# A recurrence's opening: where a background inverse is issued, and when one load is

## The chip, the cores and the metric

The kernel runs on one core of a Trainium2 chip. The metric is the device time of one execution in microseconds (us); lower is better. The engines of the core are TensorE (PE), VectorE (DVE), ScalarE (ACT), GpSimd (POOL) and SyncE (SP, which issues most DMAs). Each works through its own queue in order.

## The reference

A two-layer model on 256 time steps of width 2048, in float32. The first layer is an RWKV-7 mixer, the second a sparse attention with three branches that shares keys and values; both are followed by output projections, and a norm ends the whole. What matters here is the recurrence of the first layer, for 32 heads of 64:

```python
def wkv7_scan(r, w, k, v, a, b):
    def step(S, inp):
        r_t, w_t, k_t, v_t, a_t, b_t = inp
        sa = jnp.einsum('bhvk,bhk->bhv', S, a_t)
        S = S * w_t[:, :, None, :] + sa[..., None] * b_t[:, :, None, :] + v_t[..., None] * k_t[:, :, None, :]
        return S, jnp.einsum('bhvk,bhk->bhv', S, r_t)
    S0 = jnp.zeros((B, H, N, N), jnp.float32)
    _, o = lax.scan(step, S0, seq)
```

Its inputs r, k, v, z are products of the token-shifted, normed input with four 2048 x 2048 matrices (`a_w_rkvz`), and its output, normed by head and gated, goes through `a_w_o`.

## The kernel before

**Dense work.** All large products are done in three matmuls each: weights and activations are split into a high and a low part (`whi` by ACT at L206, `wlo` by DVE at L191), and PE adds high x high, high x low and low x high (L606 to L609 by rows, L624 to L626 by columns). `Weights` loads raw pieces on SP ahead of need and splits them in the order in which they are used.

**The recurrence in chunks.** The 256 steps are cut into four chunks of 64 (`NCH`). Within a chunk the recurrence is a triangular system; its inverse is made ahead from 32 x 32 blocks. `stage_t(b)` makes the inverse of 128 such blocks at once, one on each partition: b=0 for the first half of the heads, b=1 for the second. It doubles the block size from 1 to 32: for sizes 2 and 4 with small multiplies and adds (L832 to L846), for sizes 8 and 16 with `dot` (a multiply, L852, and a reduction, L855), after copying the solved corner transposed (L866, on ACT). At the end it stores the inverse (`tnd`, L875, on POOL), copies it transposed in four pieces (L877, ACT) and stores that (`yvd`, L879, POOL). Here b=0 is done before the recurrence begins, b=1 runs in its background.

**The loop.** U counts eight groups of four heads, v twelve slots in a group (three for each chunk: `phase(U, v // 3, v % 3)`). In a group's slots PE does the small products of the recurrence: at slot 0 the removal with mask `ama` (L1071), the bonus (L1083), at p=1 the product with the inverse (L1094, for which ACT copies X, L1089), at p=2 the outputs with the masks `amr` (L1100), the next removal and the state update (L1105). Beside them `AUX` prepares the next group U+1: B0 and B1 (transposes), G (L1021, reads A10 and Yb) at v=3, Y (L1030, reads T00) at v=4, A0 and A1 (products of keys and queries, L1054 and L1056) and the masks M2 (`ama`), M0 and M1 (`amr`), all three DVE operations of L1062, at v=10 and 11. `NORM` finishes the group before: norms, gates, and at v=10 `turn_y` (L1165). The power `rg` (L1137) is on POOL, at v=11, and `nmr`, which reads it, the first of DVE's `NORM` steps at v=1.

**Loads on POOL's queue.** `load_y(U+2, qs=(1,))` stands at v=11 ahead of `rg` and reads `yvd`; the rest of it, `qs=(0,)`, follows at v=0 of the next group, then `clear_uv`. `load_a(U+2)` stands at v=8: eight DMAs, four for A10 (L898) and four for T00 (L901) in turns. A10 and T00 have one buffer each, so a load for U+2 comes after G and Y of U+1. Both loads first require that the inverse they read is done; if it is not, the planner issues its remaining steps there.

**What sets the order.** From the recurrence on, PE, DVE, ACT, POOL and SP keep the order in which the program issues (`manual_schedule`). Between the slots `fill(n)` issues n pieces of dense work, three matmuls each, and adds their cost to a planner's clock `sch.t`. After each piece, and around each slot, `sch.pump()` gives every background generator one step if its due time has come; a step that yields a cost is due again at `sch.t` + cost, and a step of the inverse b=1 yields `PACE[0]` times its estimated length. So `PACE[0] = 0` lets each pump issue a step, and a larger pace spreads them.

**The opening.** Ahead of U=0 the preparation of group 0 is written out by hand in `PROLOGUE`: R0 and R1 (`scale_r`), a number n for `fill(n)`, G, B0, Y, B1, A0, A1, M0 to M2 as above, "I" releases the inverse b=1, and "Vn" calls `sch.pump()` n times at pace 0. The first step of the released inverse clears its tiles and asks for 1000 units of the planner's clock; A0 and A1 add 900 each to the clock, G and Y 550, B0 and B1 300, a slot 350, 200 or 700 (p=0, 1, 2) and a piece of dense work 327.

Of the kernel before, what the change touches and what calls it, by code (L numbers as in the profile page):

```python
# [12 lines left out]
AF = mybir.ActivationFunctionType  # L13
# [58 lines left out]
AUX = {2: ("B0",), 3: ("G",), 4: ("B1", "Y"), 7: ("A0",), 9: ("A1",), 10: ("T", "M2"), 11: ("M0", "M1")}  # L72
NORM = {1: ("nmr", "v", "02"), 2: ("b",), 5: ("24",), 6: ("46",), 7: ("68",), 8: ("g", "+"), 9: ("z",)}
FILLL = (3, 4, 4, 0, 0, 5, 4, 0, 4, 0, 4, 4)
PROLOGUE = ("R0", "R1", 6, "G", "B0", 4, "I", "Y", "B1", 2, "V6", "A0", 2, "A1", "M2", "V9", "V9", "M0", "M1", 2)
ZHOOK = 9
PACES, PACE = (0.6, 1.8, 3.0, 3.0), [0.0]
FILL = (3, 4, 4, 0, 0, 5, 4, 0, 4, 0, 4, 4)
FILLO, LASTFILL = 4, 36
QZ = (0, 25, 24, 1, 2, 23, 22, 21, 3, 20, 19, 18, 4, 17, 16, 15, 14, 13, 12, 11, 10)  # L80
# [137 lines left out]
def hybrid_kernel(ctx: ExitStack, tc: tile.TileContext, a: dict, out: bass.AP):  # L218
    nc = tc.nc
    V, S, G, PE = nc.vector, nc.scalar, nc.gpsimd, nc.tensor  # L220
    sch = Sched()
# [18 lines left out]
    role, turn = {}, {}  # L240
# [146 lines left out]
    W0, A0, KA, RK, KVG, BG = [prm1[:, 16 * i:16 * i + 16] for i in range(6)]  # L387
# [409 lines left out]
    def stage_t(b):  # L797
        PE, V, S, G = Ranked(nc.tensor, "stE"), Ranked(nc.vector, "stE"), Ranked(nc.scalar, "stE"), Ranked(nc.gpsimd, "stE")
        yield lambda: (8 * b + 7) in a1done and (b == 0 or "scan" in phase_done)
        A = late.tile([128, 32, 32], F32, name="invA", bufs=1)  # L800
        Tm = late.tile([128, 32, 32], F32, name="invT", bufs=1)
        M1 = late.tile([128, 16, 16], F32, name="invM", bufs=1)
        M2 = late.tile([128, 16, 16], F32, name="invM2", bufs=1)
        X = late.tile([128, 1024], F32, name="invX", bufs=1)
        nc.sync.dma_start(A.rearrange("p a b -> p (a b)"), abdd[b])
        if not b:
            V.memset(Tm, 0.0)
        if b:
            yield lambda: "inv" in phase_done
            V.memset(Tm, 0.0)  # L810
        else:
            yield 500.0
        flat = Tm.rearrange("p a b -> p (a b)")
        V.memset(flat[:, 0::33], 1.0)
        fa = A.rearrange("p a b -> p (a b)")
        V.tensor_copy(flat[:, 32::66], fa[:, 32::66])
        yield 1000.0

        pace = lambda ns: PACE[0] * (ns + 60.0) if b else 1.6 * (ns + 60.0)

        def view(t, r0, c0, n, step, rows, colsn, tr=False):
            base = t[:, r0, c0:c0 + 1]
            ap = [list(base.ap[0]), [step * 33, n], [32, rows], [1, colsn]]
            return bass.AP(tensor=base.tensor, offset=base.offset, ap=ap)

        for lv in (2, 4):
            n = 32 // (2 * lv)
            m1 = M1.rearrange("p a b -> p (a b)")[:, :n * lv * lv].rearrange("p (n i j) -> p n i j", n=n, i=lv)
            m2 = M2.rearrange("p a b -> p (a b)")[:, :n * lv * lv].rearrange("p (n i j) -> p n i j", n=n, i=lv)
            x = X[:, :n * lv * lv].rearrange("p (n i j) -> p n i j", n=n, i=lv)  # L830
            sh = [128, n, lv, lv]
            for k in range(lv):  # L832
                colA = view(A, lv, k, n, 2 * lv, lv, 1).to_broadcast(sh)
                rowT = view(Tm, k, 0, n, 2 * lv, 1, lv).to_broadcast(sh)
                V.tensor_tensor(m1 if k == 0 else x, colA, rowT, op=OP.mult)
                if k:
                    V.tensor_tensor(m1, m1, x, op=OP.add)
                yield pace((1 if k == 0 else 2) * (1.1 * n * lv * lv + 60.0))
            for k in range(lv):
                colT = view(Tm, lv, lv + k, n, 2 * lv, lv, 1).to_broadcast(sh)  # L840
                rowM = m1[:, :, k:k + 1, :].to_broadcast(sh)
                V.tensor_tensor(m2 if k == 0 else x, colT, rowM, op=OP.mult)
                if k:
                    V.tensor_tensor(m2, m2, x, op=OP.add)
                yield pace((1 if k == 0 else 2) * (1.1 * n * lv * lv + 60.0))
            V.tensor_copy(view(Tm, lv, 0, n, 2 * lv, lv, lv), m2)  # L846
        def dot(out, aa, bb, ni, nj, kk):
            x = X[:, :ni * nj * kk].rearrange("p (i j k) -> p i j k", i=ni, j=nj)
            m = 2 if b and ni * nj * kk > 512 else 1
            for i0, i1 in [(ni * n // m, ni * (n + 1) // m) for n in range(m)]:  # L850
                sh = [128, i1 - i0, nj, kk]
                V.tensor_tensor(x[:, i0:i1], aa[:, i0:i1, None, :].to_broadcast(sh), bb[:, None, :, :].to_broadcast(sh), op=OP.mult)  # L852
                if b:
                    yield pace(1.1 * (i1 - i0) * nj * kk)
                V.tensor_reduce(out[:, i0:i1], x[:, i0:i1], axis=AX.X, op=OP.add)  # L855
                yield pace(1.2 * (i1 - i0) * nj * kk) if b else pace(2.3 * ni * nj * kk + 60.0)

        TT = M2.rearrange("p a b -> p (a b)")
        M1f = M1.rearrange("p a b -> p (a b)")
        for lv in (8, 16):  # L860
            w = lv // 4
            Tt = TT[:, :lv * 16].rearrange("p (j k) -> p j k", k=lv)
            Mt = M1f[:, :lv * lv].rearrange("p (j k) -> p j k", k=lv)
            corner = [2 * lv * g for g in range(32 // (2 * lv))]
            for g, o in enumerate(corner):
                S.activation(Tt[:, g * lv:g * lv + lv], Tm[:, o:o + lv, o:o + lv].rearrange("p k j -> p j k"), AF.Copy)  # L866
            for g, o in enumerate(corner):
                for j0 in range(0, lv, w):
                    yield from dot(Mt[:, j0:j0 + w, :].rearrange("p j i -> p i j"), A[:, o + lv:o + 2 * lv, o + j0:o + lv],
                                   Tt[:, g * lv + j0:g * lv + j0 + w, j0:lv], lv, w, lv - j0)  # L870
                for i0 in range(0, lv, w):
                    yield from dot(Tm[:, o + lv + i0:o + lv + i0 + w, o:o + lv],
                                   Tm[:, o + lv + i0:o + lv + i0 + w, o + lv:o + lv + i0 + w],
                                   Mt[:, :, 0:i0 + w], w, lv, i0 + w)
        G.dma_start(tnd[b], Tm)  # L875
        for i in range(0, 32, 8):
            S.activation(A[:, i:i + 8, :], Tm[:, :, i:i + 8].rearrange("p a b -> p b a"), AF.Copy)  # L877
            yield 700.0
        G.dma_start(yvd[b], A)  # L879
        tdone.add(b)  # L880
# [5 lines left out]
    NU = NK // 2  # L886
# [53 lines left out]
    for b in range(2):  # L940
        sch.add(stage_t(b))
# [28 lines left out]
    def load_spl(U):  # L970
        for x in range(2):
            nc.sync.dma_start(SPL[U % 2][x][:, :SPW], spd[2 * U + x])

    def clear_uv(U):
        for h in range(2):
            G.memset(UV[U % 2][R[h], :, :, h, :], 0.0)
# [267 lines left out]
    PBK[1] = pair_tile(1)  # L1244
    for step in PROLOGUE:
        if isinstance(step, int):
# [16 lines left out]
    for U in range(NU):  # L1263
        PBK[U] = pair_tile(U % 2)
        P = U - 1
        PACE[0] = PACES[min(U + 1, 3)]
        for v in range(12):
            phase(U, v // 3, v % 3)
            if v % 3 == 2:
                stats(U, v // 3)  # L1270
            sch.pump()
            if v == 11:
                if U + 2 < NU:
                    load_y(U + 2, qs=(1,))
                finish(U, "rg")
            if v == 0:
                if U and U + 1 < NU:
                    load_y(U + 1, qs=(0,))
                if U + 1 < NU:
                    clear_uv(U + 1)  # L1280
                    load_v(U + 1)
                if U + 2 < NU:
                    load_spl(U + 2)
            if v == 1 and U + 1 < NU:
                scale_r(U + 1, 0)
            if v == 6 and U + 1 < NU:
                scale_r(U + 1, 1)
            if U:
                for step in NORM.get(v, ()):
                    finish(P, step)  # L1290
            for step in AUX.get(v, ()):
                if step == "T":
                    if U:
                        turn_y(P)
                elif U + 1 < NU:
                    prep(step, U + 1)
            if v == 9 and U % 4 == 0:
                load_gb(U)
            if v == 8 and U + 2 < NU:
                load_a(U + 2)  # L1300
            if v == 8:
                load_rows(vt, vd, U)
            if v == 9:
                load_rows(zt, zd, U)
            fill(FILLO if U + 1 == NU else FILLL[v] if U + 2 == NU else FILL[v])
            sch.pump()
    U = NU - 1
# [520 lines left out]
```

## Time and profile before

| | us |
|---|---|
| median of three runs | 1136.3 (1135.73 to 1138.3) |
| the profiled execution | 1137.13 |
| its span, first to last instruction | 1135.4 |
| PE busy in the span | 1111.3 |
| DVE busy | 826.1 |
| ACT busy | 726.7 |
| POOL busy | 324.4 |

The recurrence's loop begins with U=0 at 364.91 us of the span (the first L1071), U=1 follows at 395.59, U=2 at 420.13, U=3 at 445.99, U=4 at 471.86. PE's queue is in order, and its matmuls are pipelined: a dense matmul of 256 columns starts every 0.12 us at full clock, though each is drawn 0.28 us long. A row of the timeline gives start, length, engine and line, output and inputs, and in square brackets the idle time of the engine before it with the operation that ended it. In a table of stretches the columns are the stretch, its length, the busy time of PE, PEld (weight loads), DVE, ACT and POOL with the number of instructions, the granted clock of TensorE, the busy share of the DMA engines and GB/s.

### The profile page before, as it was taken

The numbers are of one execution on the slowest core, as the hardware profiler recorded it, in microseconds if no ns is written. First come the engines' busy times: TensorE is split into PE (matmuls) and PEld (weight loads), VectorE is DVE, ScalarE is ACT, GpSimd is POOL, SyncE is SP. The second block draws the span as 40 slices with busy tenths as digits, with TensorE's granted clock in tenths as the row PEclk, the third lists the DMA queues.
The fourth block names the chain that finished last, engine by engine and source line by source line (L and its number), as shares of the span: only waits on it lengthen the run. The fifth ranks groups of instructions, "written<-read, shape, count | busy, mean of one in ns | idle before, by whom it ended". The sixth has DMA issues, their size and how long they took to land.

```text
span 1135.4 us, 25694 instructions
## 1 busy us (share of the span) xinstructions
PE 1111.3 (98%) x9496; PEld 982.9 (87%) x9496; DVE 826.1 (73%) x1773; ACT 726.7 (64%) x1707; POOL 324.4 (29%) x428
## 2 busy tenths in 40 slices
PE   8999999999999999999999999999999999999997
PEld 7788899898988888898888888787989999999887
DVE  6999876689896887566677876764666877766564
ACT  7667877577764456565556766664656776766553
POOL 1300045324447465554010010100323332332012
PEclk9999999999999899999999999999999999999999
DMA  7558878877979778875568658585656365544862
GB/s 255 161 186 257 234 208 259 241 213 221 263 216 281 188 188 251 220 188 152 149 195 266 210 168 283 174 273 169 186 147 162 109 154 136 139 130 143 303 196 101
DMA packets 234463, 226.33 MB, mean 199 GB/s; under 512 B 50609, under 2 KB 184097, under 8 KB 233953
## 3 DMA queue, kind: packets, MB, share of 16 engines
q1 hardware_dynamic: 228976, 219.14, 65.4%
q0 software_dynamic: 4896, 4.95, 1.9%
q8 instruction: 75, 1.23, 0.5%
q10 hardware_dynamic: 464, 0.59, 0.1%
q14 instruction: 52, 0.42, 0.1%
HBM read 200.48 MB, written 24.15 MB: 198 GB/s over the span
## 4 chain that ended last, share of the span: by engine, by line
PE 84%; DVE 7%; issue 3%; ACT 2%; DMA 2%; POOL 1%; SPq 1%; POOLq 0%; DVEq 0%; ACTq 0%
PE bank L607 13%; PE bank L609 13%; PE bank L606 13%; PE bank L624 8%; PE bank L626 8%; PE bank L625 8%; PE bank L234 5%; DVE wlo L191 3%; PE pair L609 1%; PE pair L606 1%; PE pair L607 1%; DVE invX L852 1%; PE pair L1100 1%; PE bank L1182 1%; PE bank L774 1%
## 5 line engine op out<-in xcount | busy, mean ns | idle before, releaser
L191 DVE TENSOR_TENSOR wlo<-wraw,whi 128x512 fp32r<-128x512 f32 (+2 forms) x616 | 439.3, 726 | 163.1 <-ACT whi L206 159.3
L206 ACT ACTIVATE whi<-wraw 128x512 fp32r<-128x512 f32 (+2 forms) x664 | 403.5, 618 | 191.2 <-PE bank L609 89.3
L624 PE MATMUL bank<-mh,whi 128*128 128x256 f32 (+1 forms) x800 | 235.6, 294 | 0.4 <-ACT whi L206 0.4
L626 PE MATMUL bank<-mh,wlo 128*128 128x256 f32 (+1 forms) x800 | 228.7, 286 | 1.6 <-issue 1.6
L625 PE MATMUL bank<-ml,whi 128*128 128x256 f32 (+1 forms) x800 | 228.2, 285 | 0.0
L607 PE MATMUL bank<-wlo,mh 128*128 128x512 f32 (+3 forms) x576 | 218.0, 379 | 0.8 <-DVE wlo L191 0.7
L609 PE MATMUL bank<-whi,ml 128*128 128x512 f32 (+3 forms) x576 | 215.2, 376 | 0.0
L606 PE MATMUL bank<-whi,mh 128*128 128x512 f32 (+3 forms) x576 | 190.3, 377 | 0.6 <-ACT Vt L1472 0.3
L624 PEld LDWEIGHTS bank<-mh,whi 128*128 128x128 f32 (+1 forms) x800 | 152.1, 190 | 5.8 <-ACT whi L206 1.0
L625 PEld LDWEIGHTS bank<-ml,whi 128*128 128x128 f32 (+1 forms) x800 | 152.4, 191 | 1.6
L626 PEld LDWEIGHTS bank<-mh,wlo 128*128 128x128 f32 (+1 forms) x800 | 152.1, 190 | 1.2
L607 PEld LDWEIGHTS bank<-wlo,mh 128*128 128x128 f32 x576 | 108.3, 188 | 17.9 <-DVE wlo L191 1.8
L609 PEld LDWEIGHTS bank<-whi,ml 128*128 128x128 f32 x576 | 108.3, 188 | 16.1
L606 PEld LDWEIGHTS bank<-whi,mh 128*128 128x128 f32 x576 | 107.0, 188 | 17.1 <-ACT Vt L1472 0.7
L191 POOL TENSOR_TENSOR wlo<-wraw,whi 128x512 fp32r<-128x512 f32 (+2 forms) x48 | 57.4, 1196 | 187.1 <-ACT whi L206 164.0
L607 PE MATMUL bank<-wlo,kvh 128*128 128x512 f32 x192 | 76.9, 401 | 0.0
L609 PE MATMUL bank<-whi,kvl 128*128 128x512 f32 x192 | 76.1, 396 | 0.0
L606 PE MATMUL bank<-whi,kvh 128*128 128x512 f32 x192 | 67.4, 396 | 0.0
L420 ACT ACTIVATE mh<-mtmp 128x256 fp32r<-128x256 f32 x95 | 37.8, 411 | 17.7 <-DVE mtmp L427 16.4
L427 DVE SCALAR_TENSOR_TENSOR mtmp<-xx,prm,xn 128x256 f32<-128x256 f32 x95 | 46.5, 501 | 0.1
L607 PEld LDWEIGHTS bank<-wlo,kvh 128*128 128x128 f32 x192 | 36.1, 188 | 8.7 <-issue 0.4
L609 PEld LDWEIGHTS bank<-whi,kvl 128*128 128x128 f32 x192 | 36.1, 188 | 7.4
(350 smaller groups left out, 1927.7 us busy)
## 6 DMA issues: line engine op xcount, KB each, us to landing
wraw<-in_a_w_rkvz_dram SPq DMA_DIRECT2D x128, 512.0 KB, 5.3
wraw<-in_kv_w_dram SPq DMA_DIRECT2D x48, 512.0 KB, 4.4
wraw<-in_b_w_in_dram SPq DMA_DIRECT2D x40, 512.0 KB, 4.2
wraw<-in_a_w_o_dram SPq DMA_DIRECT2D x32, 512.0 KB, 4.5
wraw<-in_b_w_o_dram SPq DMA_DIRECT2D x32, 512.0 KB, 3.8
spd<-sp SPq DMA_DIRECT2D x16, 642.0 KB, 5.2
spl<-spd SPq DMA_DIRECT2D x16, 642.0 KB, 6.9
wraw<-in_b_w_in_dram SPq DMA_DIRECT2D x24, 384.0 KB, 3.3
```

Source lines behind the costliest of these rows:

```text
L191: eng.tensor_tensor(lv, src, hv.bitcast(F32), op=OP.subtract)
L206: self.nc.scalar.activation(hv, src, AF.Copy)
L234: return fn(*args, **kw)
L420: S.activation(h, src, AF.Copy)
L427: V.scalar_tensor_tensor(m, xx[:, k, :], mu[:, k:k + 1], xn[:, k, 1:], op0=OP.mult, op1=OP.add)
L606: PE.matmul(o, mh[:, ts], wh[:, 0, :], start=k == ends[0], stop=False)
L607: PE.matmul(o, mh[:, ts], wl[:, 0, :], start=False, stop=False)
L609: PE.matmul(o, ml[:, ts], wh[:, 0, :], start=False, stop=k == ends[1])
L624: PE.matmul(o, wh[:, s, :], mh, start=k == 0 and first, stop=False, **kw)
L625: PE.matmul(o, wh[:, s, :], ml, start=False, stop=False, **kw)
L626: PE.matmul(o, wl[:, s, :], mh, start=False, stop=k == NK - 1, **kw)
L774: PE.matmul(ab[r, c * 64:c * 64 + 64], c3(at)[r, c, :], BK[r, c, h, :], start=True, stop=True)
```

## The change

In the prologue the pumps V6 and twice V9 go; ten (V10) stand between the fill behind A0 and A1, so that no inverse step is issued between M2, M0 and M1. The pace after "I" is 0 instead of 0.6, that of U=1 2.2 instead of 3.0. At v=2 of U=0 nine pumps are called at pace 0. The transposed copies of the inverse b=1 go from ACT to DVE. At U=2, `load_a(4)` moves from v=8 to v=11, where it stands behind `load_y(4, qs=(1,))`, `rg`, M0 and M1.

```diff
-PROLOGUE = ("R0", "R1", 6, "G", "B0", 4, "I", "Y", "B1", 2, "V6", "A0", 2, "A1", "M2", "V9", "V9", "M0", "M1", 2)
+PROLOGUE = ("R0", "R1", 6, "G", "B0", 4, "I", "Y", "B1", 2, "A0", 2, "V10", "A1", "M2", "M0", "M1", 2)
 ZHOOK = 9
-PACES, PACE = (0.6, 1.8, 3.0, 3.0), [0.0]
+PACES, PACE = (0.0, 1.8, 2.2, 3.0), [0.0]
...
+        turn = V.tensor_copy if b else lambda o, i: S.activation(o, i, AF.Copy)
         for lv in (8, 16):
...
-                S.activation(Tt[:, g * lv:g * lv + lv], Tm[:, o:o + lv, o:o + lv].rearrange("p k j -> p j k"), AF.Copy)
+                turn(Tt[:, g * lv:g * lv + lv], Tm[:, o:o + lv, o:o + lv].rearrange("p k j -> p j k"))
...
+            if U == 0 and v == 2:
+                PACE[0] = 0.0
+                for _ in range(9):
+                    sch.pump()
+                PACE[0] = PACES[1]
...
-            if v == 8 and U + 2 < NU:
+            if v == (11 if U == 2 else 8) and U + 2 < NU:
                 load_a(U + 2)
```

## The prediction

> **What bounds the kernel now.** I read the page first (busy time, the 40 slices), then the busy time of each engine by stretches of the recurrence, then the timeline of each engine around the stretches that stand out.
>
> ```profile
> PE 1111.3 (98%) x9496; PEld 982.9 (87%) x9496; DVE 826.1 (73%) x1773; ACT 726.7 (64%) x1707; POOL 324.4 (29%) x428
> PEclk9999999999999899999999999999999999999999
> 364.91:395.59 30.68, 26.96 (x465) 24.19 (x466) 24.76 (x86) 12.05 (x33) 14.24 (x27) 0.83 0.79 204
> 471.86:495.47 23.61, 23.42 (x495) 21.30 (x494) 15.28 (x41) 14.18 (x41) 14.88 (x24) 1.00 0.67 170
> 371.10:381.34 10.24, 9.06 (x108) 7.75 (x107) 8.17 (x28) 3.17 (x9) 2.75 (x6) 0.50 0.93 289
> ```
>
> TensorE (PE) runs nearly all the time, in program order, so a microsecond that PE waits is a microsecond of the span. One slice of the clock row dips. In the rows of stretches (length, busy PE, PEld, DVE, ACT, POOL, then the granted clock) the first turn of the recurrence, U=0, takes 30.68 us, and U=4, which does the same dense work, 23.61. So **U=0 has some 7.1 us too many**, and its clock of 0.83 says that part of it is a slow clock: 0.50 for 10.24 us.
>
> ```profile
> 364.91 0.54 PE L1071 MATMUL pair<-uv,ama 128*64 128x64 f32 x8
> 367.00 0.28 PE L626 MATMUL bank<-mh,wlo 128*128 128x256 f32 x1
> 369.82 0.34 PE L1094 MATMUL pair<-X,Yb 64*64 64x64 f32 x8 [2.54 <-ACT X L1089]
> 369.09 0.51 ACT L866 ACTIVATE invM<-invT 128x64 f32<-128x64 f32 x2 [6.49 <-DVE invT L846]
> 369.51 0.26 ACT L1089 ACTIVATE X<-pair 128x128 f32<-128x128 f32 x1
> 364.72 0.18 DVE L842 TENSOR_TENSOR invM<-invT,invM 128x32 f32<-128x32 f32 x1
> 368.48 0.23 DVE L844 TENSOR_TENSOR invM<-invM,invX 128x64 f32<-128x64 f32 x1
> 371.51 1.28 DVE L1062 TENSOR_TENSOR amr<-pair,cst 128x512 f32<-128x512 f32 x2
> ```
>
> In the timeline (start, length, instruction, idle time before it) PE stops for 2.54 us at 367.28, for the copy X (L1089). ACT could have made X at about 366, but ahead of X in its queue stand the two transposed copies of the background inverse (L866), and these wait for eighteen small VectorE (DVE) operations (364.72 to 368.71). The half clock begins at 371.10, 3.8 us after PE stopped. The output masks (amr, L1062) come last of all, at 371.51.
>
> **The change, part by part.** I worked the planner's clock through by hand, since it decides at build time where each inverse step is issued.
>
> *Prologue.* The V6 of before issues nothing: the first step after "I" asks for 1000 units and its time has not come. By the start of U=0 the old order has issued 23 steps, the new one 15: three, then V10, then two. V10 ends exactly with the last step of block size 4. Behind it come A1, M2, M0, M1, and only then the transposed copies, now on DVE. So X no longer waits for the inverse: the 2.54 us go, and with them the late masks and the slow clock, 7.1 us at most. What is late next is the first mask, ama.
>
> ```profile
> 360.50 0.83 POOL L1012 TENSOR_TENSOR ars<-spl 128x384 f32<-128x384 f32 x1
> 361.43 0.83 POOL L1012 TENSOR_TENSOR ars<-spl 128x384 f32<-128x384 f32 x1
> 360.52 0.87 DVE L837 TENSOR_TENSOR invM<-invM,invX 128x32 f32<-128x32 f32 x1
> 364.11 0.69 DVE L1062 TENSOR_TENSOR ama<-bank,cst 128x512 f32<-128x512 f32 x1 [2.73 <-PE bank L1056]
> ```
>
> The hole that V10 is to fill is the 2.73 us ahead of ama, from 361.39. The ten steps took 364.72 to 368.71, so 3.99 us: 1.3 us longer than the hole. Moreover an operation of this size took 0.87 us instead of 0.19 while GpSimd (POOL) multiplied for 0.83 (360.50), and a second such product stands at 361.43, in the hole. Without that clash ama ends at 361.4 + 4.0 + 0.7 = 366.1, with it at 366.9, and PE, which starts L1071 at 364.91 now, waits 1.2 or 2.0 us. I take 2.0, since the one row of such a meeting shows DVE as the loser. **Opening: 7.1 - 2.0 = 5.1 us gained**, 5.9 at best.
>
> *The second turn's inputs.* G of U=1 now comes near 374.1 (366.9 + the 7.2 us from L1071 to L1021 in U=3, 445.99 to 453.16); the last of its loads left at 365.51.
>
> ```profile
> L898 POOL DMA_DIRECT2D a<-abd x4: 548/548/577, 362.2 to 365.5; - x4
> DMA to landing us min/median/max: 5.9/6.7/7.1
> ```
>
> Landed by 372.6: hidden, by 1.5 us. If POOL instead loses the clash, these loads move back by up to 4 us and G waits 2.5, while ama gains 0.8; I take nothing.
>
> *Nine pumps at U=0, v=2.* The pump just before them issues a step that is due 235 units later (1.8 x (1.1 x 64 + 60)); the nine do not advance the clock. They issue nothing, and I cost them at nothing.
>
> *The copies on DVE.* Three copies of about 0.3 us (0.51 for two on ACT) go to DVE. Nothing waits for them but the inverse.
>
> *The rest dealt out.* U=0 issues 33 steps instead of 29, U=1 14 instead of 11, and the last reduction moves from v=6 of U=2 to v=8. DVE is busy 24.76 us in U=0 now; V10's 4.0 go out of it and four late steps of about 0.6 as well, which leaves some 18.5 of 23.6 us: room enough. At v=8 of U=2 the reduction (0.67 us by its like) comes ahead of the chain that ends at L1165, for which PE waits already:
>
> ```profile
> 441.74 0.69 PE L1165 MATMUL pair<-cst,O 64*64 64x64 f32 x32 [0.20 <-DVE O L1154]
> 432.46 0.68 DVE L855 TENSOR_REDUCE invT<-invX 128x32 f32<-128x512 f32 x1
> ```
>
> 0.6 us lost there, and I add 0.3 for U=1: **0.9 us lost**, between 0 and 1.5.
>
> *The load moved from v=8 to v=11 of U=2.* This is the costly part. load_a(4) brings A10, which G of U=4 reads at v=3 of U=3. Here is the queue of now:
>
> ```profile
> 437.94 2.35 ACT L877 ACTIVATE invA<-invT 128x256 f32<-128x256 f32 x4
> 442.50 0.66 ACT L1168 ACTIVATE mh<-pair 128x256 fp32r<-128x256 f32 x2 [0.29 <-PE pair L1165]
> 443.04 0.64 ACT L206 ACTIVATE whi<-wraw 128x512 fp32r<-128x512 f32 x1
> 440.58 0.54 POOL L879 DMA_DIRECT2D yvd<-invA  x1 [4.24 <-ACT invA L877]
> 441.12 0.57 POOL L898 DMA_DIRECT2D a<-abd  x1
> 444.40 0.55 POOL L898 DMA_DIRECT2D a<-abd  x1
> 445.89 1.63 POOL L909 DMA_DIRECT2D Yb<-yvd  x3 [0.39 <-DMA t<-tnd]
> 448.07 0.55 POOL L909 DMA_DIRECT2D Yb<-yvd  x1 [0.55 <-DMA t<-tnd]
> 448.63 1.68 POOL L1137 TENSOR_TENSOR rg<-rg,half 128x8 f32<-128x8 f32 x1
> 450.35 0.17 DVE L1144 SCALAR_TENSOR_TENSOR nmr<-mv,rg 128x8 f32<-128x8 f32 x1 [0.98 <-POOL rg L1137]
> 453.16 1.31 PE L1021 MATMUL pair<-Yb,a 64*64 64x32 f32 x31
> 453.68 0.68 PEld L1021 LDWEIGHTS pair<-Yb,a 64*64 64x64 f32 x27 [0.22 <-DMA Yb<-yvd]
> yvd<-invA POOLq DMA_DIRECT2D x1, 512.0 KB, 3.7
> a<-abd POOLq DMA_DIRECT2D x4, 16.0 KB, 4.7
> ```
>
> G already takes its operands as they land: it stops at 453.68 for Yb. In the new order the four copies L877 fall to v=9, 10, 10 and 11; the last ends about 445.6 (443.16, the end of L1168, + three copies of 0.59 + one split of 0.64). POOL then issues the store yvd at 445.9 and is blocked, because load_y(4) reads what the store writes: landed at 449.6 (3.7 us). Today the eight loads of load_a lie over that landing; now nothing does. Then four loads Yb (2.2 us) to 451.8, the power rg (1.7) to 453.5, and only now load_a: its last part for A10 is the seventh issue, 6 x 0.55 us on, at 456.8, landed 4.7 later at 461.5. Some 0.5 us more by the waits within Yb and the late chain before: 462.0. **G runs 8.3 us later than 453.68.** Behind the blocked store stand rg, and behind rg DVE's nmr and the next state copy, some 3 us late; G's wait covers this. Bounds: were there no wait for the landing, 458.1 (4.4 us); with a landing of 6.5 us, as the store of the first inverse took, and 6.3 for the last load, 466.5 (13 us).
>
> ```profile
> L879 POOL DMA_DIRECT2D yvd<-invA x2: 537/538/538, 290.9 to 440.6; - x2
> DMA to landing us min/median/max: 3.7/5.1/6.5
> L898 POOL DMA_DIRECT2D a<-abd x8: 548/551/577, 441.1 to 463.2; - x8
> DMA to landing us min/median/max: 3.9/5.1/6.3
> ```
>
> *The clock after that wait.* 2.54 us of idle PE halved the clock; 8.3 us will. The 10.24 us at 0.50 held 9.06 us of busy PE, so cost 4.5. After G the small products are followed by dense ones with few holes; I take 3 us, between 0 and 4.5.
>
> The row fits three windows of 3.41 us (10.24), which is what the Trainium skill, "TensorE: Matmul & The Clock Gate", Part 1, gives as the window of the activity monitor. By its rule one busy window restores the clock, which by that estimate would cost 1.7 us and make the sum 1.3 lower; here 10.24 us passed, with 1.18 us of holes in them. Its other rule, no gap over about 3 us, does not hold here: 2.54 us was enough.
>
> **Sum.** -5.1 + 0.9 + 8.3 + 3.0 = +7.1 us. The profiled execution took 1137.1 us (span 1135.4), 0.8 over the median of 1136.3; the terms are differences, so I set them on the median: **1143.4 us**.
>
> **The rivals.**
>
> *The late load is short and the opening wins* (other side). G's last operand at 458.1 (4.4 us), PE's own holes in U=3 and U=2 shrink beside it, no slow clock, and POOL loses the clash, so 5.9 gained: with 0.9 lost and 2 of holes recovered, -5.9 + 4.4 + 0.9 - 2 = -2.6, 1133.7. It decides where G's last load lands before about 459. For it: the holes exist,
>
> ```profile
> 434.13 0.28 PE L626 MATMUL bank<-mh,wlo 128*128 128x256 f32 x1 [1.59 <-issue]
> ```
>
> against it: the order on POOL, and the row in which G waits today. Chance 0.17.
>
> *Both even out*: 4.4 late, a short slow clock of 1.5, 5.9 gained, 0.9 lost: +0.9, 1137.2; decided by whether the store's landing is waited for. 0.10.
>
> *The clock halves in the prologue too*: 2.0 us of idle PE lies between 1.59, which left the clock at full, and 2.54, which did not. Then 4 us of the opening's gain stay away: 1147.4. 0.15.
>
> *The nine pumps do issue*: nine small steps (2.3 us of DVE), the inverse ends some five slots earlier, the store has landed by v=11, and the late load costs 4.6 instead of 8.3: 1139.7. It needs a due time that my working of the planner excludes. 0.03.
>
> **How the numbers follow.** The forecast holds 0.55, with its bounds from 1139.5 (G 4.4 late) to 1148.1 (G 13 late). Range with the others: 1133 to 1150. A measurement of this kernel can tell about 0.2% (2.3 us) from no change: slower 0.73 (forecast, prologue clock, nine pumps), same 0.10, faster 0.17.
>
> **What would show it.** Right: X (L1089) copied within 1 us of L1083 in U=0, PE's wait there at L1071 for ama, 1.2 to 2 us; U=0 near 24 to 26 us at full clock; the copies L877 beside v=9 to 11 of U=2; POOL idle before L909 for the store; L898 behind L1137; PE waiting at L1021 of U=3 for a<-abd, and a second dip of the clock. Wrong: G(4) without a wait of over 3 us, L1071 on time, or a burst of nine steps at v=2.

## The result, and the profile after

The changed kernel took 1148.32 us (median of four runs, 1145.39 to 1150.55) beside 1136.01 us for the kernel before (1135.68 to 1138.3): a ratio of 1.0097, with a 95% interval of 1.0079 to 1.0115. It is slower by about 1%. The profiled execution took 1148.43 us, with a span of 1146.7; before it was 1137.13.

From here on the lines of the changed code are one further than before (the removal is L1072, the bonus L1084, X L1090, G L1022, the masks L1063, the store yvd L880, the loads L899 and L902, Yb L910, rg L1138), and `turn_y` is L1166.

First the page of the changed kernel, its busy times and its clock row; then its stretches (length, busy PE, PEld, DVE, ACT, POOL, granted clock, DMA share, GB/s) for the turns U=0, U=3 and U=4, and for its two stretches at half clock.

```profile
PE 1113.1 (97%) x9496; PEld 984.6 (86%) x9496; DVE 827.3 (72%) x1776; ACT 725.4 (63%) x1704; POOL 324.1 (28%) x428
PEclk9999999999999999899999999999999999999999
```

```profile
368.13:393.33 25.20, 25.20 (x462) 23.16 (x462) 19.29 (x69) 11.06 (x30) 12.82 (x23) 0.88 0.86 221
444.22:482.78 38.56, 27.20 (x496) 24.28 (x494) 15.31 (x41) 14.01 (x41) 20.13 (x36) 0.82 0.65 173
482.78:506.30 23.52, 23.41 (x495) 21.40 (x494) 15.77 (x39) 13.92 (x41) 13.92 (x24) 1.00 0.74 199
367.44:374.27 6.83, 6.13 (x65) 5.69 (x66) 6.03 (x20) 1.97 (x5) 4.13 (x8) 0.50 1.19 242
456.20:469.85 13.65, 6.93 (x105) 6.06 (x106) 1.18 (x5) 3.10 (x11) 5.78 (x12) 0.50 0.81 192
```

The clock row still has one 8, but it has moved three slices on: the prologue's dip is now short, and a larger one has come in U=3. That turn takes 38.56 us, 15.0 more than U=4, and PE is busy in it for 27.20 only. In U=0 PE has no hole left (25.20 of 25.20), yet the clock is halved for 6.83 us, 6.14 of them in U=0.

To follow where the time goes, take the start of the bonus products, one marker in each turn. Each number is the distance to the next marker in one profiled execution.

| turn | before | changed | difference |
|---|---|---|---|
| up to U=0 | 365.38 | 368.85 | +3.47 |
| U=0 | 30.52 | 24.97 | -5.55 |
| U=1 | 24.56 | 24.54 | -0.02 |
| U=2 | 25.92 | 26.35 | +0.43 |
| U=3 | 25.87 | 38.46 | +12.59 |
| U=4 to the end | 664.88 | 665.26 | +0.38 |

The sum is +11.30 us, the difference of the two executions. The opening gains 2.1 us (3.47 - 5.55), and U=3 loses 12.6.

The opening in the timeline of the changed kernel (start, length, instruction, idle time before it):

```profile
362.15 0.84 POOL L1013 TENSOR_TENSOR ars<-spl 128x384 f32<-128x384 f32 x1
362.15 0.88 DVE L842 TENSOR_TENSOR invM<-invT,invM 128x32 f32<-128x32 f32 x1
363.08 0.83 POOL L1013 TENSOR_TENSOR ars<-spl 128x384 f32<-128x384 f32 x1
363.20 0.77 DVE L844 TENSOR_TENSOR invM<-invM,invX 128x32 f32<-128x32 f32 x1
367.35 0.68 DVE L1063 TENSOR_TENSOR ama<-bank,cst 128x512 f32<-128x512 f32 x1
368.13 0.78 PE L1072 MATMUL pair<-uv,ama 128*64 128x64 f32 x8 [3.24 <-issue]
369.97 0.28 ACT L1090 ACTIVATE X<-pair 128x128 f32<-128x128 f32 x1 [5.97 <-PE pair L1084]
```

X no longer waits for the inverse: it is copied as soon as the bonus products are there. In its place PE waits 3.24 us for the first mask, `ama`, which ends at 368.03. (The row says "issue", since the profile shows no semaphore that ended the wait; the mask's end 0.1 us before is what identifies it.) The steps in front of the mask met both POOL products, and each meeting stretched an operation of about 0.2 us to 0.8 or 0.9. The clock was halved 2.6 us after PE had stopped at 364.89.

The second wait, in the timelines of POOL, ACT and PE:

```profile
441.91 1.80 ACT L878 ACTIVATE invA<-invT 128x256 f32<-128x256 f32 x3
444.01 0.54 POOL L880 DMA_DIRECT2D yvd<-invA  x1 [5.61 <-ACT invA L878]
449.30 2.21 POOL L910 DMA_DIRECT2D Yb<-yvd  x4 [4.75 <-DMA yvd<-invA]
451.52 1.68 POOL L1138 TENSOR_TENSOR rg<-rg,half 128x8 f32<-128x8 f32 x1
453.15 0.59 POOL L899 DMA_DIRECT2D a<-abd  x1
456.53 0.55 POOL L899 DMA_DIRECT2D a<-abd  x1
```

```profile
455.25 0.46 PE L1088 MATMUL pair<-S,ars 64*64 64x64 f32 x16 [3.97 <-DVE sta L1125]
459.69 0.39 PE L1022 MATMUL pair<-Yb,a 64*64 64x32 f32 x2 [3.97 <-DMA a<-abd]
461.52 0.71 PE L1022 MATMUL pair<-Yb,a 64*64 64x32 f32 x4 [1.44 <-DMA t<-tnd]
464.02 0.95 PE L1022 MATMUL pair<-Yb,a 64*64 64x32 f32 x25 [1.79 <-DMA a<-abd]
```

Read it downward. The last copy of the inverse ends at 443.71, its store leaves at 444.01, and POOL then stands for 4.75 us because `load_y` needs what the store writes. Only then come Yb, the power `rg` and the late load. PE waits first for the state copy, which is queued on VectorE behind `nmr` and so behind `rg` (3.97 us), and then three times for parts of the load. G takes its last operand 19.31 us after the bonus of U=3 (464.02 - 444.71); before the change it was 7.30 us (453.68 - 446.38).

### The profile page after: what moved, and what is told of

Its sections match the earlier page's. It is cut to its first block, busy times and chain, and to the rows that moved or that the text cites. A ratio compares the mean times of both kernels' runs of the same rounds, so it can differ in the third digit from the quotient of the medians.

```text
span 1146.7 us, 25692 instructions
## 1 busy us (share of the span) xinstructions
PE 1113.1 (97%) x9496; PEld 984.6 (86%) x9496; DVE 827.3 (72%) x1776; ACT 725.4 (63%) x1704; POOL 324.1 (28%) x428
## 3 DMA queue, kind: packets, MB, share of 16 engines
q8 instruction: 75, 1.23, 0.5%
## 4 chain that ended last, share of the span: by engine, by line
PE 84%; DVE 8%; issue 3%; ACT 2%; DMA 1%; POOL 1%; POOLq 0%; DVEq 0%; SPq 0%; ACTq 0%
PE bank L607 13%; PE bank L609 13%; PE bank L606 13%; PE bank L624 8%; PE bank L626 8%; PE bank L625 8%; PE bank L234 5%; DVE wlo L191 3%; PE pair L609 1%; PE pair L606 1%; PE pair L607 1%; DVE invX L852 1%; PE pair L1101 1%; ACT whi L206 1%; PE bank L1183 1%
## 5 line engine op out<-in xcount | busy, mean ns | idle before, releaser
L421 DVE TENSOR_TENSOR ml<-mtmp,mh 128x256 fp32r<-128x256 f32 x95 | 40.8, 445 | 2.7 <-ACT mh L420 2.5
```

The costliest lines, as they stand in the source:

```text
L421: V.tensor_tensor(l, src, h.bitcast(F32), op=OP.subtract)
```

## The experiments

All runs compare with the kernel before on the same chip. Each kernel left one profiled execution, and its turns are set beside each other here, measured as above.

| kernel | U=0 | U=1 | U=2 | U=3 | ratio to before, 95% interval |
|---|---|---|---|---|---|
| before | 30.52 | 24.56 | 25.92 | 25.87 | |
| changed | 24.97 | 24.54 | 26.35 | 38.46 | 1.0097 (1.0079 to 1.0115) |
| e1_load_v8 | 23.11 | 24.54 | 26.86 | 29.40 | 1.0033 (1.0020 to 1.0046) |
| e2_only_load_v11 | 28.86 | 24.55 | 24.88 | 33.78 | 1.0083 (1.0068 to 1.0097) |
| e3_load_first | 24.43 | 24.88 | 26.20 | 31.31 | 1.0039 (1.0024 to 1.0053) |
| e4_v4_v6 | 26.10 | 25.24 | 27.10 | 30.40 | 1.0041 (1.0026 to 1.0057) |
| e5_paces | 24.13 | 25.04 | 28.58 | 25.17 | 1.0003 (0.9991 to 1.0014) |
| e6_v5 | 23.51 | 26.26 | 27.23 | 25.48 | 0.9985 (0.9974 to 0.9995) |
| e7_turn_only | 29.14 | 24.54 | 24.60 | 25.56 | 1.0013 (1.0001 to 1.0024) |
| e8_paces2 | 23.92 | 25.95 | 26.36 | 25.33 | 0.9993 (0.9979 to 1.0007) |
| e9_paces3 | 24.77 | 28.12 | 25.71 | 24.50 | 1.0004 (0.9989 to 1.0019) |

### The late load: three kernels

**e1_load_v8**, from the changed kernel:

```diff
-            if v == (11 if U == 2 else 8) and U + 2 < NU:
+            if v == 8 and U + 2 < NU:
```

> The changed kernel with load_a(4) back at v=8 of U=2; nothing else differs. Theory A (the load's place alone makes the second wait): the G of U=4 takes its operands as before, the 12.6 us that the changed kernel loses between the bonus of U=2 and that of U=4 go, the 2.1 us of the opening less 0.4 in U=2 stay: 1136.0 - 1.7 = 1134.3 us. Theory B (the inverse that ends later costs too, since its store leaves at 444.0 in place of 440.6 and load_y has to wait for its landing): the store lands about 448.7, the four loads Yb leave by 451.0, G takes its last operand 5.1 us later as before, so near 456 in place of 452.0: some 4 us of the loss stay, 1138.3 us. G then waits for Yb, not for a.

Median 1138.32 us beside 1135.23 for the kernel before. POOL and PE in its timeline, and its half clock:

```profile
435.97 0.54 POOL L880 DMA_DIRECT2D yvd<-invA  x1 [1.76 <-ACT invA L878]
442.86 0.55 POOL L910 DMA_DIRECT2D Yb<-yvd  x1 [1.55 <-DMA a<-abd]
447.02 2.22 POOL L910 DMA_DIRECT2D Yb<-yvd  x4
```

```profile
449.12 0.46 PE L1088 MATMUL pair<-S,ars 64*64 64x64 f32 x16 [1.39 <-DVE sta L1125]
450.99 0.71 PE L1022 MATMUL pair<-Yb,a 64*64 64x32 f32 x25 [0.45 <-DMA Yb<-yvd]
```

```profile
451.30:458.14 6.84, 6.84 (x99) 6.21 (x93) 1.15 (x4) 3.85 (x11) 0.23 (x2) 0.50 0.94 277
```

The time is theory B's, but the agreement to 0.1 us is luck, since two of its steps are not as it said. G is 2.5 us late and not 4, and the store leaves at 435.97, not at 444.0. `load_a` requires the inverse to be done, so with the load at v=8 the planner issues the remaining copies there in one burst. (The burst has a price of its own: X stands behind the four copies on ScalarE, and PE waits 1.42 us for it in U=2.) Moving the load to v=11 had therefore moved two things, the load and the end of the inverse. Even so the loads and Yb come later than before, G takes its last operand 9.82 us after the bonus of U=3 (at 441.17) in place of 7.30, 1.39 us of it a wait for the state copy, and 6.84 us at half clock follow: U=3 is 3.5 us longer than before.

**e2_only_load_v11**, from the kernel before:

```diff
-            if v == 8 and U + 2 < NU:
+            if v == (11 if U == 2 else 8) and U + 2 < NU:
```

> The kernel before with only load_a(4) moved from v=8 to v=11 of U=2; the inverse ends as before and its store has landed by v=11, with no load lying over the landing that was needed. Theory A (order on POOL alone): Yb leaves up to 448.6, rg ends at 450.3, the seventh load leaves at 453.6 and lands 4.7 to 7.4 us later, 458.3 to 461: G 4.6 to 7.3 us late, and up to 3 us of slow clock: 1140.6 to 1146, likeliest 1142. Theory B (the late store is the larger part): POOL, which no longer has eight loads between the store and load_y, is done with load_y earlier, about 446.5 to 447.5 as the store has landed at 444.3, rg at 449, and the load costs 3 us or less without a slow clock: 1137 to 1139.

Median 1143.53 us. The line numbers here are those of the kernel before.

```profile
439.39 0.54 POOL L879 DMA_DIRECT2D yvd<-invA  x1 [5.40 <-ACT invA L877]
443.35 2.21 POOL L909 DMA_DIRECT2D Yb<-yvd  x4 [3.42 <-DMA yvd<-invA]
447.25 0.59 POOL L898 DMA_DIRECT2D a<-abd  x1
450.92 0.55 POOL L898 DMA_DIRECT2D a<-abd  x1
457.86 0.95 PE L1021 MATMUL pair<-Yb,a 64*64 64x32 f32 x25 [1.05 <-DMA a<-abd]
```

Theory A: the load's new place alone costs most of the change's loss. G's last operand comes 13.83 us after the bonus of U=3, 6.5 later than before. The store's landing, which the eight loads covered, is now waited for (3.42 us), as theory B had not reckoned.

The changed kernel's 12.0 us (19.31 - 7.30) can be read off against this one. From the bonus of U=3 (444.03 here, 444.71 there) the store leaves at -4.64 here and at -0.70 in the changed kernel: 3.9 us. Its landing holds POOL 1.3 us longer (4.75 for 3.42). With the 6.5 us of the load's place that is 11.7. The last load took longer to G, 7.5 us in place of 6.9, and in e2_only_load_v11 the loads themselves stood for 0.4 us on the queue, which the changed kernel's did not.

**e3_load_first**, from the changed kernel:

```diff
+                if U == 2:
+                    load_a(U + 2)
...
-            if v == (11 if U == 2 else 8) and U + 2 < NU:
+            if v == 8 and U != 2 and U + 2 < NU:
```

> The changed kernel with load_a(4) at v=11 of U=2 ahead of load_y(4) in place of behind it and rg. Theory A (place behind the landing, load_y and rg): the eight loads leave from 444.6 to 449, over the landing of the store; then Yb to 451.5. A10 lands by 454.5, Yb by 456: G waits to 456 in place of 464, so 8 us of the loss come back and the time is about 1140 us, 1138 to 1141. Rival (it is the late inverse, wherever the load stands): within 2 us of the changed kernel's 1148.

Median 1139.17 us, theory A.

```profile
442.27 0.57 POOL L899 DMA_DIRECT2D a<-abd  x1
447.23 2.17 POOL L910 DMA_DIRECT2D Yb<-yvd  x4
453.15 0.46 PE L1088 MATMUL pair<-S,ars 64*64 64x64 f32 x16 [4.13 <-DVE sta L1125]
454.22 1.17 PE L1022 MATMUL pair<-Yb,a 64*64 64x32 f32 x27 [0.38 <-DMA Yb<-yvd]
```

At the same slot, with the same late inverse, swapping two groups of DMAs on one queue brings back 7.2 us of U=3. The loads now lie over the store's landing: POOL has no wait there (442.27 to 447.23 without a stop, but for 0.58 us within the loads), and G waits for Yb (0.38 us) and no longer for a. G is still 4.5 us later than before, 11.77 us after the bonus of U=3, and nearly all of that is the wait ahead of it: `rg`, behind the loads and Yb, ends at 451.10, `nmr` follows it on VectorE, and PE stands 4.13 us for the state copy.

### The opening: two kernels and a part by itself

**e4_v4_v6**, from e1_load_v8:

```diff
-PROLOGUE = ("R0", "R1", 6, "G", "B0", 4, "I", "Y", "B1", 2, "A0", 2, "V10", "A1", "M2", "M0", "M1", 2)
+PROLOGUE = ("R0", "R1", 6, "G", "B0", 4, "I", "Y", "B1", 2, "A0", 2, "V4", "A1", "M2", "M0", "M1", "V6", 2)
```

> The kernel e1_load_v8 with the ten inverse steps of the prologue divided: four ahead of A1 and six behind M1. Theory A (the ten steps hold up the first mask, and PE's wait for it halves the clock): the mask comes some 2.5 us sooner, PE waits 0.7 us in place of 3.24 at the first removal and the clock stays at full through U=0: 2.5 + 3.4 = 5.9 us less than e1_load_v8, and U=0 takes about 23.6 to 24.5 us from its bonus to the next. Rival (the half clock comes from elsewhere, for instance from the current that the dense work draws after the hole, or the late masks amr hold up the outputs): PE still waits or the dip of the clock stays, within 2.5 us of e1_load_v8.

Median 1139.63 us, 1.3 above e1_load_v8, well within the two intervals: the rival's time. The first removal starts without any wait, as theory A wanted, but a new wait stands further on:

```profile
363.88 0.68 DVE L1063 TENSOR_TENSOR ama<-bank,cst 128x512 f32<-128x512 f32 x1
371.31 0.41 DVE L1011 TENSOR_TENSOR mb<-bank,spl 128x256 f32<-128x256 f32 x1
371.78 0.55 PE L1041 MATMUL bank<-cst,spl 128*128 128x128 f32 x3 [1.84 <-DVE mb L1011]
372.28:375.68 3.40, 3.40 (x49) 3.18 (x47) 3.23 (x13) 1.73 (x5) 2.72 (x6) 0.50 1.15 334
```

The six steps behind M1 and the ones that follow at pace 0 are now ahead of `mb`, an operation that prepares the next group. PE waits for that, and 3.4 us at half clock follow. That is the rival's late operation on VectorE, if another one than it named; no run here speaks for the current that it also names.

**e7_turn_only**, from the kernel before, makes one part of the change by itself:

```diff
+        turn = V.tensor_copy if b else lambda o, i: S.activation(o, i, AF.Copy)
...
-                S.activation(Tt[:, g * lv:g * lv + lv], Tm[:, o:o + lv, o:o + lv].rearrange("p k j -> p j k"), AF.Copy)
+                turn(Tt[:, g * lv:g * lv + lv], Tm[:, o:o + lv, o:o + lv].rearrange("p k j -> p j k"))
```

> The kernel before with only the transposed copies of the inverse moved from ScalarE to VectorE. X no longer stands behind them and the product that reads X comes at about 367. Theory A (the late output masks are the second half of the same wait, so the copies alone gain nothing): amr still comes at 371.5 or later, PE waits 3 to 4 us for it at the output product of U=0 in place of 2.5 us for X, and the time is within 1.5 us of the kernel before. Rival (X was what cost it): PE's wait of U=0 falls under 1 us, the clock stays at full, and the time is 3 to 5 us lower.

Median 1136.6 us beside 1135.55, ratio 1.0013. Theory A:

```profile
370.21 1.28 DVE L1063 TENSOR_TENSOR amr<-pair,cst 128x512 f32<-128x512 f32 x2
371.04 0.30 PE L1101 MATMUL pair<-uv,amr 128*64 128x64 f32 x2 [2.27 <-DVE amr L1063]
374.10 0.90 PE L1041 MATMUL bank<-cst,spl 128*128 128x128 f32 x3 [1.64 <-DVE mb L1011]
```

The product that reads X comes at 366.81, 2.5 us after the bonus in place of 4.4, and PE then stops for the output masks (2.27 us, less than the 3 to 4 of theory A) and for `mb`. Freeing ScalarE alone moves the wait to the next operation in VectorE's queue.

**e6_v5**, from e5_paces (below), puts five steps in place of ten ahead of A1:

```diff
-PROLOGUE = ("R0", "R1", 6, "G", "B0", 4, "I", "Y", "B1", 2, "A0", 2, "V10", "A1", "M2", "M0", "M1", 2)
+PROLOGUE = ("R0", "R1", 6, "G", "B0", 4, "I", "Y", "B1", 2, "A0", 2, "V5", "A1", "M2", "M0", "M1", 2)
```

> The kernel e5_paces with five inverse steps ahead of A1 in place of ten, and none behind M1. Theory A (PE's wait for the first mask is the length of those steps, and a short wait leaves the clock alone): PE waits at the first removal 0 to 0.8 us in place of the 1.23 to 3.24 us of the traces with ten, no half clock in U=0; 1.5 to 4 us less than e5_paces. Rival (as in e4_v4_v6, the steps only come later and hold up another operation of VectorE, mb for one, that PE waits for in U=0): a wait of 1 us or more elsewhere in U=0, within 1.5 us of e5_paces.

Median 1133.72 us, ratio 0.9985 (0.9974 to 0.9995): the only kernel of the study that is shown to be faster than the kernel before, 1.7 us below e5_paces, though the two intervals just overlap. It is theory A, at its lower end: PE waits 0.58 us, and U=0 runs at full clock:

```profile
365.91 0.54 PE L1072 MATMUL pair<-uv,ama 128*64 128x64 f32 x8 [0.58 <-issue]
365.91:389.46 23.55, 23.20 (x462) 21.06 (x462) 20.60 (x74) 10.49 (x30) 14.06 (x26) 1.00 1.02 264
411.52 0.69 PE L1166 MATMUL pair<-cst,O 64*64 64x64 f32 x32 [1.51 <-DVE O L1155]
421.92 0.55 PE L1041 MATMUL bank<-cst,spl 128*128 128x128 f32 x3 [0.98 <-DVE mb L1011]
```

It gives part of this back in U=1 and U=2, where VectorE is late with O and with `mb`.

### When the inverse ends: three kernels

**e5_paces**, from e1_load_v8:

```diff
-PACES, PACE = (0.0, 1.8, 2.2, 3.0), [0.0]
+PACES, PACE = (0.0, 1.4, 2.0, 2.0), [0.0]
```

> The kernel e1_load_v8 with the inverse's paces 0, 1.4, 2.0, 2.0 in place of 0, 1.8, 2.2, 3.0; by the planner's clock the last step of the inverse then falls at v=5 of U=2 in place of v=8. Theory A (what is left of the second wait in e1_load_v8 is the late end of the inverse, with its four copies and its store just ahead of the loads): the store lands before v=8, the loads leave as early as before the change or earlier, G of U=4 waits no longer than before, and U=2 with U=3 take 50 to 52 us in place of 56.3; with the opening's gain the time is 3 to 5 us below e1_load_v8, some 1 to 3 us below the kernel before. Rival (VectorE, fuller in U=0 and U=1 by some 3 us of steps, now delays PE there): the gain of U=3 is given back in U=0 to U=2, and the time stays within 1.5 us of e1_load_v8.

Median 1135.41 us, ratio 1.0003; some 3 us below e1_load_v8 (their ratios, each to the kernel before on its own chip, are 1.0033 and 1.0003) but not below the kernel before. Theory A is right about U=3: 25.17 us, with no row of waiting at G at all. The rival is right that the gain is paid for in part, though its time, within 1.5 us of e1_load_v8, is missed. U=2 takes 28.58 us: three waits between 421 and 426, of 0.52 and 0.47 us for VectorE and of 0.79 us for X, which now stands behind a copy of the inverse on ScalarE, are followed by 6.82 us at half clock.

```profile
421.50 0.55 PE L1041 MATMUL bank<-cst,spl 128*128 128x128 f32 x3 [0.52 <-DVE mb L1011]
425.77 0.34 PE L1095 MATMUL pair<-X,Yb 64*64 64x64 f32 x8 [0.79 <-ACT X L1090]
426.30:433.12 6.82, 6.82 (x90) 6.09 (x88) 1.49 (x5) 4.87 (x13) 0.81 (x2) 0.50 0.99 320
```

**e8_paces2** and **e9_paces3**, from e6_v5, deal the steps out more to U=0:

```diff
-PACES, PACE = (0.0, 1.4, 2.0, 2.0), [0.0]
+PACES, PACE = (0.0, 0.8, 2.6, 2.2), [0.0]
```

> The kernel e6_v5 with the inverse's paces 0, 0.8, 2.6, 2.2 in place of 0, 1.4, 2.0, 2.0: three steps more in U=0, some three fewer in U=1, the end at the same slot of U=2. Theory A (what e6_v5 loses, 26.26 us for U=1 and 27.23 us for U=2 against 24.56 and 25.92 before, is VectorE's queue, too full there): U=1 falls to 24.5 to 25.2 us and the time to 1 to 2 us below e6_v5, 2.5 to 4 us below the kernel before. Rival (U=0 is just as full): U=0 rises from 23.5 us by as much, no change against e6_v5.

```diff
-PACES, PACE = (0.0, 1.4, 2.0, 2.0), [0.0]
+PACES, PACE = (0.0, 0.6, 3.0, 3.0), [0.0]
```

> The kernel e6_v5 with paces 0, 0.6, 3.0, 3.0: five steps more in U=0, and the pace of before in U=1 and U=2, so that the inverse ends at v=8 of U=2 as before, where load_a requires it. Theory A: U=0 about 23.6 to 24.5 us, U=1 and U=2 as before (24.5 and 25.9 us), U=3 as before (25.9 us): the opening's gain of 5 to 7 us of U=0 stays nearly whole, 3 to 5 us below the kernel before. Rival (VectorE in U=0 too full, as in e7_turn_only and e4_v4_v6, where PE waited 1.6 and 1.8 us for mb): a wait for mb in U=0 with a half clock, level with the kernel before.

Neither theory held as it was put. U=0 stays short in both (23.92 and 24.77 us, no half clock), but U=1 hardly becomes shorter in the first (25.95 us for 26.26) and longer in the second: 28.12 us in e9_paces3, where the wait for `mb` that the rival put into U=0 stands at the beginning of U=1.

```profile
396.89 0.55 PE L1041 MATMUL bank<-cst,spl 128*128 128x128 f32 x3 [2.16 <-DVE mb L1011]
```

In e9_paces3 U=3 takes 24.50 us, less than in any other kernel, and the time is still level with the kernel before (1135.78 us for both). The medians of e6_v5 and e8_paces2 (1133.72 and 1134.76) cannot be told apart.

## Why the prediction was right, and where it was off

The forecast was slower, 1143.4 us in a range of 1133 to 1150; the median is 1148.32. The sign and the mechanism hold. The sum of +7.1 us against +11.3 in the two profiled executions divides like this.

| term | predicted | changed kernel's trace |
|---|---|---|
| the opening, to U=1 | -5.1 (with the clock's rival -1.1) | -2.1 |
| U=1 and U=2 | +0.9 | +0.4 |
| G of U=4 late | +8.3 | +12.0 |
| the clock after it, and the rest of U=3 | +3.0 | +0.6 |
| U=4 to the end | 0 | +0.4 |

The forecast had the opening 3.0 us and G 3.7 us too low, and the clock 2.4 and the two turns 0.5 too high. Errors of both signs cancel in part, and that part of the agreement is luck. The median lies just above the bound that the forecast itself had (1148.1, with G 13 us late), and inside the range.

**The nine pumps** issue nothing, as reckoned: without them every engine gets the same instructions in the same order.

**The step that failed in the opening** is the end of the mask at 366.9 with a wait of 2.0 us and a clock that stays up. The mask ended at 368.03 and PE waited 3.24 us; U=0 with its 25.20 us lies within the predicted 24 to 26, but not at full clock. Two things were mis-sized: the steps of the inverse that stand ahead of the mask started at 362.15 and not at 361.39, and POOL's products met two operations, not one. What turned the term is the clock, the case given 0.15. The kernels that kept ten steps ahead of A1 show how near the edge this is. With the same program up to there they waited 3.24 (changed), 1.23 (e1_load_v8), 2.69 (e3_load_first) and 2.91 us (e5_paces), and the half clock that followed lasted 6.83, 0, 3.41 and 3.41 us. The kernel before is no steadier: 10.24 us at half clock in its trace, 3.41 in that of e2_only_load_v11, which has the same opening. So the 7.1 us too many that the prediction read from one trace of U=0 were a long case. Over the traces U=1 begins at 391.65 on average with the changed U=0 (393.82, 389.77, 391.37) and at 395.25 with the old one (395.90, 394.60): a gain of 3.6 us, between forecast and rival.

**The load.** Its whole chain came as the prediction put it: the copies of the inverse at v=9 to 11, POOL stopped at Yb for the store, `rg` behind it, the load behind `rg`, and PE waiting at G for a. Put on the scale of before (1.67 us later, by the bonus of U=3), the store left at 445.7, where 445.9 was forecast. Mis-sized were the two landings. The store's was taken as 3.7 us and POOL went on 5.3 us after its issue; the load's was taken as 4.7 and G went on 7.5 us after the last issue for A10 (456.53 to 464.02). That is 1.6 and 2.8 us more; less the 0.5 that had been added for waits it makes, within 0.2 us, the step from 8.3 to 12.0. By the profile's own count the store landed after 4.7 us, in place of 3.7 (POOL went on 0.6 us behind that), and the four loads of A10 after 6.4 to 7.4, where the old order has 3.9 to 5.7. The medians came from the whole page and from U=2 of the old order, where the queue of loads was spread out; the upper ends that stood as the bound (6.5 and 6.3 us) were nearer, and for the load still too low.

**The clock after it** was to cost 3 us, and 0.6 are left over. The row at half clock is long, 13.65 us, but 7.82 us of it lie ahead of G's last operand, where PE mostly waits (1.10 us busy). From that operand to the bonus of U=4 the stretches are, before and changed:

```profile
453.68:472.25 18.57, 17.07 (x375) 15.37 (x375) 8.99 (x25) 9.73 (x29) 8.27 (x16) 1.00 0.93 232
464.02:483.17 19.15, 18.95 (x373) 17.12 (x373) 9.15 (x26) 9.69 (x28) 8.35 (x16) 0.85 0.43 108
```

PE is busy 1.9 us longer with the same work, which by this count is what the clock cost, and idle for 0.20 us in place of 1.50: 1.3 us of holes went, which the prediction had reckoned with only in its rival of the other side. In e1_load_v8, e2_only_load_v11 and e3_load_first PE is busy 2.3, 2.7 and 2.3 us longer there and the same 1.3 us of holes go, so that 1.0, 1.4 and 1.0 us are left over. A slow clock costs only what PE has to do in it.

**U=1 and U=2** cost 0.4 in place of 0.9: `turn_y` waits 0.79 us for O at U=2, 0.59 more than before, and U=1 takes as long as before.

**The late store** was the part that was not seen for what it is. The prediction dated the copies at v=9 to 11 but did not say that it was the load's own requirement that had made them end by v=8, nor priced that by itself. The kernels divide it: the load's place alone makes G 6.5 us late, a later end of the inverse with the load at v=8 2.5, both together 12.0. They add to more than their sum because the load at v=8 also forces the inverse to end there: by the bonus of U=3 the store leaves at -5.20 in e1_load_v8 and at -0.70 in the changed kernel.

What stays open: the median of e1_load_v8 lies 3.1 us above the kernel before, while its turns, with the average opening, account for some 0.9 (-3.6 in the opening, +0.9 in U=2, +3.5 in U=3); with one trace for each kernel, here the fastest of its nine executions, that rest can't be placed. Nor was it tried why the four loads of A10 landed after 2.1 to 3.4 us in e3_load_first, 3.9 to 5.7 in the kernel before, 5.6 to 5.8 in e1_load_v8 and 6.4 to 7.4 in the changed kernel. Their medians, from 2.8 to 6.7 us, differ by more than the 2.8 us by which the prediction had that term too low.

## What to carry to other kernels

A load that stands between a store and the reader of that store pays for itself by covering the landing; before moving it back, look at what POOL would wait for in its place, and at what the load's own requirement forces to be finished. Freeing one engine from background steps helps only if the next operation in the other engine's queue is not late too: count what is queued ahead of every operation that TensorE reads, up to the next turn. And where a clock changes from execution to execution, read a stretch's excess from more than one trace before taking it as a term.

## What the runs showed of the hardware

**Half clock comes in whole windows.** Around these waits the traces of the eleven kernels show thirteen stretches at half clock, none of them in e6_v5, e8_paces2 and e9_paces3 (edges from the granted clock), and each lasted 3.41 us or a whole multiple of it within 0.02: once in five of them, twice in five (6.82 to 6.84), three times in two (10.24) and four times in one (13.65). Three of the rows, two from e3_load_first and one from e2_only_load_v11:

```profile
368.54:371.95 3.41, 3.41 (x23) 3.07 (x21) 3.24 (x13) 1.17 (x3) 2.59 (x5) 0.50 1.18 239
453.86:460.70 6.84, 6.48 (x103) 5.85 (x104) 1.49 (x5) 3.77 (x12) 1.63 (x4) 0.50 1.13 285
455.30:465.54 10.24, 8.30 (x111) 7.41 (x111) 1.15 (x4) 3.85 (x11) 3.26 (x7) 0.50 0.67 183
```

The length of a wait alone does not decide: 2.16 us at L1041 in e9_paces3 left the clock at full, 1.84 us at the same line in e4_v4_v6 halved it, and in e5_paces three short waits within 5 us were enough. The Trainium skill, "TensorE: Matmul & The Clock Gate", Part 1, says that the window runs freely and does not start with the work; that agrees with the opening of the kernel before, where waits of 2.54 and 2.42 us in two traces were followed by three windows and by one. The ten steps ahead of A1 can't show it, since there the longer waits had the more windows. Its rule that one busy window restores the clock agrees with the rows of 3.41 us, but not with e1_load_v8 and e5_paces, where the profile shows PE busy for all of 6.84 and 6.82 us at half clock.

**GpSimd and VectorE met more often than one row had shown.** In the changed kernel each of the two POOL products of 0.83 us stretched a small VectorE operation from 0.2 to 0.77 or 0.88 us; which operation it is changes from trace to trace, and in e7_turn_only and e8_paces2 there is no such meeting.
